# State space mixer: step sizes in the exponents, rows and their exponentials fetched on GpSimd's queue, all groups in one strand

## The chip, the cores and the metric

One core of one Trainium2 chip runs the whole kernel in one launch. The metric is the device time of one execution in microseconds (us); lower is better. Time of before: 1747.45 us, the median of 3 runs (1746.28 to 1748.42). The engines are PE (TensorE, matmuls), DVE (VectorE), ACT (ScalarE), POOL (GpSimd) and SP (SyncE, which here only issues transfers). PEld is PE's loading of weights. Each engine carries out its own instructions in the order in which they stand in its program; an instruction that must wait holds up those behind it.

## The reference

Two layers of a hybrid block over 256 latent and 256 context tokens (D_MODEL 1024): a shared input projection, a bidirectional state space mixer and an attention mixer beside each other, gates, an output projection, and a feed-forward part. The change touches only the state space mixer, in chunks of 128 tokens, with 16 heads in 4 groups. Per direction it computes:

```python
xd = (xs * dt[..., None]).reshape(bsz, nc, SSD_CHUNK, g, r, p)
a = (dt * a_head).reshape(bsz, nc, SSD_CHUNK, g, r).transpose(0, 3, 4, 1, 2)
a_cs = jnp.cumsum(a, axis=-1)
cb = jnp.einsum('bclgn,bcsgn->bgcls', cc, bc)
decay_in = jnp.exp(segsum(a))
y_diag = jnp.einsum('bgcls,bgrcls,bcsgrp->bclgrp', cb, decay_in, xd)
...
y_off = jnp.einsum('bclgn,bcgrpn,bgrcl->bclgrp', cc, h_in, jnp.exp(a_cs))
y = (y_diag + y_off).reshape(bsz, n, n_heads, p)
```

Here a is the step size times a negative number, and segsum gives a_cs[l] - a_cs[s] where s <= l and minus infinity elsewhere. So the output of a chunk is a part inside the chunk (the matrix cb * decay * dt, applied to xs) and a part from the state h_in that enters it. The second direction does the same on the reversed tokens; both are summed.

## The kernel before, in words

**Matrix products.** Every large product is done with both operands split into a high and a low part (three matmuls for one). Weight blocks of 128x1024 come by SP's queue (load_w, L304), ACT casts the high part whi (L313), DVE subtracts for the low part wlo (L314). `gemm_f` (L393 to L410) runs the matmuls of a block and calls `pump()` after every 6 of them. `pump()` moves two lists of generators, `lanes[0]` and `lanes[1]`, on by one step each. Whatever such a step issues to PE is kept at that place of PE's program (`pmm`, `ptr`, L84 to L88). The instructions of the other engines are put in order by a scheduler, ahead of time; they need not follow the order of the code.

**The state space stage.** In each layer it runs beside 10 blocks of GEMM columns: four blocks XS (the input xs, evacuated with a 3-tap convolution, L568 to L572, and a gate by tanh, L665 and L666), two blocks GS, four blocks Z. Layer 0 has 4 chunks of 128 (N = 512), layer 1 has 2 (N = 256); with 4 groups that is 16 and 8 items (group g, chunk t).

**States** (`states`, in lane 0, one generator per group): transposes xs and B to xT (psssT, L910) and bT, then six times: xd = xT * ddt on POOL (L925), a matmul psstate, and the new state h = h * etot + psstate on DVE (L935, L938) or a copy on ACT (L933).

**Outputs** (`outputs`, in lane 1, one generator per group, started when its states have xT). An item's cumulative sums a_cs stand as rows in DRAM (csd, written on POOL's queue at L861). `fetch` brings eight rows, broadcast to all 128 partitions: 512 KB by SP's queue (L952, two buffers). `head` then does: the product pscb on PE; its copy under the two triangular masks, cbm (DVE L961); cc = exp(cs) (ACT L966); cs minus the column's own sums csc (POOL L969, once for each direction); their minimum (DVE L972) and its exponential E (ACT L974); cc * CF (DVE L975). The item's own step then makes X: per head, cbm times the step size of the one direction (ACT L991) plus cbm times that of the other (DVE L992), and then X * E (DVE L993). The 12 (or 8, where a direction has no state coming in) matmuls pyyd take xT with X and h_in with cc.

Of the 2 buffers for cs, one is free again when E has been used in X * E.

**Around it.** Before the stage, a small part computes the step sizes dt, ddt, csc, csd and etot for all heads of a layer (L822 to L864); the attention, gates and the attention's output projection lie between it and the stage.

## Time and profile before

| | |
|---|---|
| median of 3 runs | 1747.45 us (1746.28 to 1748.42) |
| the profiled execution, its own time | 1740.01 us |
| its span (first to last instruction) | 1738.2 us |
| mean granted clock of PE | 0.993 |
| PE / DVE / ACT / POOL busy | 96% / 66% / 49% / 10% |
| state space stage of layer 0 | 406.8 to 577 us of the span |
| state space stage of layer 1 | 1346.4 to 1477 us |
| 512 KB fetches cs<-csd | 24, on SP's queue, median 5.8 us from issue to landing |

How the rows of the profile are read. A row of a group: line, engine, operation, output<-inputs, shapes, count | busy us, mean ns of one | idle time of the engine just before them, and who ended it. A row of a tile: ns min/median/max, first and last start. A row of the waits: who waited for whom, us in total, times, longest. A row of the windows: the stretch, its length, busy us of PE, PEld, DVE, ACT, POOL (with counts), the granted clock, the share of the DMA engines, GB/s. A row of the timeline: start, duration, engine, line, and in brackets the idle time before it and who ended it. A row of the transfers: issuing queue, count, KB each, median us to landing. A few per cent of the matmul records are missing.

### The profile page before, as it was taken

How to read it: one execution, taken by the hardware profiler on the slowest of the kernel's cores; microseconds unless marked ns; L12 is line 12 of the kernel's file. 1: busy time of each engine (PE TensorE's matmuls, PEld its weight loads, DVE VectorE, ACT ScalarE, POOL GpSimd, SP SyncE). 2: the span in 40 equal slices, each digit the busy share in tenths (PEclk: the TensorE clock that was granted, in tenths of full speed). 3: DMA queues.
4: the chain of work that ended last, by engine and by line, in shares of the span. 5: the costliest groups of instructions: out<-in, count | busy, mean ns of one | idle time of the engine just before them, and what ended most of it. 6: DMA issues, size and time to landing. Idle time of an engine off the chain costs nothing. (4 is left out here: it accounts for less than half of the span.)

```text
span 1738.2 us, 27022 instructions
## 1 busy us (share of the span) xinstructions
PE 1667.1 (96%) x10547; PEld 1406.2 (81%) x10547; DVE 1148.0 (66%) x2008; ACT 848.2 (49%) x1567; POOL 181.3 (10%) x212
## 2 busy tenths in 40 slices
PE   7999999999988999999999999999999898989997
PEld 4788878777766788888888888788879788989997
DVE  4776667325988855766666326666675789779964
ACT  3565665413545423644444225555655455466653
POOL 3000010001433000300000002100000252010000
PEclk9999999999999999999999999999999999989999
DMA  9644333555443234233323335844535445646653
GB/s 317 215 127 126 115 119 108 166 173 146 121 107 100 74 109 146 74 97 97 97 87 95 92 108 161 255 146 146 152 93 171 121 110 144 199 154 185 193 176 117
DMA packets 233199, 240.71 MB, mean 138 GB/s; under 512 B 10908, under 2 KB 223551, under 8 KB 233071
## 3 DMA queue, kind: packets, MB, share of 16 engines
q1 hardware_dynamic: 230720, 237.14, 45.4%
q8 instruction: 83, 1.36, 0.3%
q0 software_dynamic: 1312, 1.03, 0.2%
q10 hardware_dynamic: 1039, 0.81, 0.1%
q14 instruction: 45, 0.37, 0.1%
HBM read 234.62 MB, written 4.33 MB: 137 GB/s over the span
## 5 line engine op out<-in xcount | busy, mean ns | idle before, releaser
L314 DVE TENSOR_TENSOR wlo<-raw,whi 128x1024 fp32r<-128x1024 f32 (+1 forms) x318 | 388.3, 1221 | 255.7 <-ACT whi L313 254.8
L313 ACT CAST whi<-raw 128x1024 fp32r<-128x1024 f32 (+1 forms) x318 | 329.2, 1036 | 378.4 <-PE pmmmm L408 146.6
L407 PE MATMUL pmmmm<-th,whi 128*128 128x512 f32 x744 | 306.3, 412 | 1.6 <-DVE chv L572 1.6
L408 PE MATMUL pmmmm<-tl,whi 128*128 128x512 f32 x744 | 296.5, 399 | 0.0
L409 PE MATMUL pmmmm<-th,wlo 128*128 128x512 f32 x744 | 295.6, 397 | 0.0
L407 PEld LDWEIGHTS pmmmm<-th,whi 128*128 128x128 f32 x744 | 140.5, 189 | 42.2 <-issue 7.9
L409 PEld LDWEIGHTS pmmmm<-th,wlo 128*128 128x128 f32 x744 | 140.4, 189 | 34.5 <-issue 1.0
L408 PEld LDWEIGHTS pmmmm<-tl,whi 128*128 128x128 f32 x744 | 140.5, 189 | 31.0 <-issue 2.2
L393 PE MATMUL pmmmm<-th,whi 128*128 128x256 f32 x480 | 138.5, 289 | 1.5 <-ACT whi L313 1.3
L395 PE MATMUL pmmmm<-th,wlo 128*128 128x256 f32 x480 | 134.7, 281 | 0.6 <-DVE wlo L314 0.6
L394 PE MATMUL pmmmm<-tl,whi 128*128 128x256 f32 x480 | 134.8, 281 | 0.0
L969 POOL TENSOR_TENSOR cs<-cs,csc 128x512 f32<-128x512 f32 x48 | 69.1, 1454 | 264.0 <-DMA cs<-csd 141.5
L393 PEld LDWEIGHTS pmmmm<-th,whi 128*128 128x128 f32 x480 | 90.7, 189 | 6.2 <-issue 3.8
L394 PEld LDWEIGHTS pmmmm<-tl,whi 128*128 128x128 f32 x480 | 90.8, 189 | 0.7 <-issue 0.4
L395 PEld LDWEIGHTS pmmmm<-th,wlo 128*128 128x128 f32 x480 | 90.6, 189 | 0.8 <-DVE wlo L314 0.8
L409 PE MATMUL psmm<-th,wlo 128*128 128x512 f32 x200 | 79.3, 397 | 0.0
L725 ACT ACTIVATE e<-psscore,nmx 128x512 f32<-128x512 f32 (+1 forms) x96 | 58.1, 610 | 43.5 <-DVE nmx L722 40.5
L408 PE MATMUL psmm<-tl,whi 128*128 128x512 f32 x200 | 79.2, 396 | 0.0
L521 POOL TENSOR_TENSOR rs<-ms,mhalf 128x2 f32<-128x2 f32 x9 | 6.3, 699 | 698.5 <-DVE ms L518 698.5
L407 PE MATMUL psmm<-th,whi 128*128 128x512 f32 x200 | 79.0, 395 | 0.0
L722 DVE TENSOR_REDUCE nmx<-psscore 128x1 f32<-128x512 f32 (+1 forms) x80 | 51.8, 684 | 34.3 <-PE psscore L85 34.2
L441 PE MATMUL pmmmm<-whi,th 128*128 128x256 f32 x256 | 74.3, 290 | 0.0
(346 smaller groups left out, 3899.0 us busy)
## 6 DMA issues: line engine op xcount, KB each, us to landing
raw<-in_w_in_dram SPq DMA_DIRECT2D x124, 512.0 KB, 4.0
raw<-in_w_up_dram SPq DMA_DIRECT2D x88, 512.0 KB, 3.6
mraw<-in_w_mod_dram SPq DMA_DIRECT2D x80, 512.0 KB, 4.7
raw<-in_w_down_dram SPq DMA_DIRECT2D x45, 512.0 KB, 3.6
cs<-csd SPq DMA_DIRECT2D x24, 512.0 KB, 5.8
boot<-in_w_mod_dram SPq DMA_DIRECT2D x16, 512.0 KB, 9.3
raw<-in_w_br_att_dram SPq DMA_DIRECT2D x16, 512.0 KB, 3.6
raw<-in_w_br_ssd_dram SPq DMA_DIRECT2D x16, 512.0 KB, 3.5
```

The costliest lines, as they stand in the source:

```text
L313: pin(A.copy(hi[:, 0:n, :], raw[:, 0:n, :]))
L314: pin(V.tensor_tensor(lo[:, 0:n, :], raw[:, 0:n, :], hi[:, 0:n, :].bitcast(F32), op=ALU.subtract))
L393: T.matmul(o[f], whi[:, kk, cs], xh, start=first, stop=False)
L394: T.matmul(o[f], whi[:, kk, cs], xl, start=False, stop=False)
L395: T.matmul(o[f], wlo[:, kk, cs], xh, start=False, stop=last)
L407: T.matmul(o, whi[:, k % 4, cs], hi[k][:, 0:n], start=k == 0, stop=False)
L408: T.matmul(o, whi[:, k % 4, cs], lo[k][:, 0:n], start=False, stop=False)
L409: T.matmul(o, wlo[:, k % 4, cs], hi[k][:, 0:n], start=False, stop=k == k_tiles - 1)
L441: T.matmul(b[:, n, :], hi[k][:, ts], whi[:, k % 4, :], start=k == 0 and n == 0, stop=False)
L722: V.tensor_reduce(nmx[:, cc, 0:ng], sc[cc].rearrange("p (g k) -> p g k", g=ng), axis=AX.X, op=ALU.max, negate=True)
L725: A.activation(e[cc][:, g * w:(g + 1) * w], sc[cc][:, g * w:(g + 1) * w], AF.Exp, bias=nmx[:, cc, g:g + 1], accum_out=sm[:, cc, g:g + 1])
L969: G.tensor_tensor(cs[:, dr], cs[:, dr], csc[:, t, 16 * dr + 4 * g:16 * dr + 4 * g + 4].unsqueeze(2).to_broadcast([P, 4, P]), op=ALU.subtract)
```

## The change

1. **Step sizes in the exponents.** csc becomes ln(max(dt, 1e-37)) minus the column's cumulative sum. Per direction, exp(row + csc) is then dt times the decay. The triangular masks become `far`, a tile with 0 inside and -1e30 outside, made once, which POOL adds to the fetched rows (new L979, once for each direction). ACT takes the exponentials head by head with csc as bias, 8 of 128x128 (new L985), and copies pscb to cb (new L981). DVE adds the two directions (new L998) and makes X by one product with cb (new L999).
2. **Two tables in DRAM.** Beside csd's rows their exponentials (ecr) are written; cc is fetched ready-made and only multiplied by CF (DVE, new L1001). A layer's writes on POOL's queue go from 8 to 16 in layer 0 and stay 8 in layer 1.
3. **GpSimd's queue.** Both fetches, 512 KB each, are issued from POOL (new L970): the rows with three buffers and three items ahead, the exponentials with two buffers and two items ahead.
4. **One strand.** One `outputs` generator goes through all items of the layer and is started before the XS blocks; it waits before an item's output matmuls until that group's states are done.
5. **States in pairs.** Both directions' xd are issued in one step, 11 steps rather than 14 for a group.

```diff
-        csd = dp.tile([4, 2, 16, P], F32, name=f"csd{i}")
+        csd = [dp.tile([4, 2, 16, P], F32, name=f"csd{i}_{n}") for n in range(2)]
...
+            V.tensor_scalar(u, dtT[:, :, 0:32], 1e-37, None, op0=ALU.max)
+            A.activation(u, u, AF.Ln)
...
-                V.tensor_copy(csc[:, :, cs], p1v[:, dr, :, cs])
+                V.tensor_tensor(csc[:, :, cs], u[:, :, cs], p1v[:, dr, :, cs], op=ALU.subtract)
...
+            A.activation(ecr, p3[:, 0:256], AF.Exp)
-            for t in range(4):
+            for t in range(NT):
...
-                    G.dma_start(csd[t, dr], csr[r:r + 16, dr * P:(dr + 1) * P])
+                    for n, src in enumerate((csr, ecr)):
+                        G.dma_start(csd[n][t, dr], src[r:r + 16, dr * P:(dr + 1) * P])
...
-                cs = up.tile([P, 2, 4, P], F32, tag="cs", name=nm("cs"), bufs=2)
-                nc.sync.dma_start(cs.rearrange("p d h l -> p d (h l)"),
+                d = up.tile([P, 2, 4, P], F32, tag=("cs", "cc")[n], name=nm("rows"), bufs=(3, 2)[n])
+                G.dma_start(d.rearrange("p d h l -> p d (h l)"),
...
-                V.tensor_tensor(cbm, cb[:, 0:P].unsqueeze(1).to_broadcast([P, 2, P]), tri2, op=ALU.mult)
-                A.activation(cc[:, d0:d1], cs[:, d0:d1], AF.Exp)
                 for dr in range(2):
-                    G.tensor_tensor(cs[:, dr], cs[:, dr],
-                                    csc[:, t, 16 * dr + 4 * g:16 * dr + 4 * g + 4].unsqueeze(2).to_broadcast([P, 4, P]),
-                                    op=ALU.subtract)
-                V.tensor_tensor(cs[:, 0], cs[:, 0], cs[:, 1], op=ALU.min)
-                A.activation(E, cs[:, 0], AF.Exp)
+                    G.tensor_tensor(cs[:, dr], cs[:, dr], far[:, dr, :].unsqueeze(1).to_broadcast([P, 4, P]), op=ALU.add)
+                A.copy(cb, pc[:, 0:P])
+                for dr in range(2):
+                    for h in range(4):
+                        c = 16 * dr + 4 * g + h
+                        A.activation(cs[:, dr, h, :], cs[:, dr, h, :], AF.Exp, bias=csc[:, t, c:c + 1])
...
-                for h in range(4):
-                    A.activation(X[:, h, :], cbm[:, 0, :], AF.Copy, scale=dcol[0])
-                    V.scalar_tensor_tensor(X[:, h, :], cbm[:, 1, :], dcol[1], X[:, h, :], op0=ALU.mult, op1=ALU.add)
-                V.tensor_tensor(X, X, E, op=ALU.mult)
+                V.tensor_tensor(cs[:, 0], cs[:, 0], cs[:, 1], op=ALU.add)
+                V.tensor_tensor(X, cs[:, 0], cb.unsqueeze(1).to_broadcast([P, 4, P]), op=ALU.mult)
+                V.tensor_tensor(ccv, ccv, CF[g][:, tsl].unsqueeze(1).to_broadcast([P, 4 * len(dirs), P]), op=ALU.mult)
+                if n + 3 < len(items):
+                    sums.append(fetch(*items[n + 3], 0))
...
+                if n + 2 < len(items):
+                    grown.append(fetch(*items[n + 2], 1))
...
+        lanes[1].append(outputs())
         for g in range(4):
...
-            lanes[1].append(outputs(g, sh))
```

**How the instructions move.** Three places. First, GpSimd at the start of layer 0's stage. Before: the subtractions of items 0 and 1 (cs_4044, cs_4067), then xd of group 0.

```order
L969 TENSOR_TENSOR cs_4044<-cs_4044,csc_622 128x512 [waits DMAHW2_49,DMAHW3_49,DMAHW1_49,DMAHW4_49,DMAHW0_49,DMAHW5_49,DVE_49,DMAHW6_49,PE_49,DMAHW7_49,Activation_49,Pool_49]
L969 TENSOR_TENSOR cs_4044<-cs_4044,csc_622 128x512
L969 TENSOR_TENSOR cs_4067<-cs_4067,csc_622 128x512 [waits DMAHW4_49,Activation_49]
L969 TENSOR_TENSOR cs_4067<-cs_4067,csc_622 128x512
L925 TENSOR_TENSOR xd_4040<-xT_4008,ddt_624 128x256 [waits DVE_49]
L925 TENSOR_TENSOR xd_4083<-xT_4008,ddt_624 128x256
L925 TENSOR_TENSOR xd_4122<-xT_4008,ddt_624 128x256 [waits PE_49]
```
After, from the mask additions of item 2 on (rows_3939): rows_3975 and rows_4295 are the rows of items 3 and 4, of which the first waits for X of item 0 and the second for X of item 1 (DVE); xd_4099 is the first xd of group 0.

```order
L979 TENSOR_TENSOR rows_3939<-rows_3939,far 128x512 [waits DMASW6_49]
L979 TENSOR_TENSOR rows_3939<-rows_3939,far 128x512
L970 DMA rows_3975<-csd_0_625 128x2x512 [waits DMASW1_49,DVE_49,DMASW2_49,Activation_49,Pool_49]
L970 DMA rows_4295<-csd_0_625 128x2x512 [waits DVE_49,Activation_49,Pool_49]
L979 TENSOR_TENSOR rows_3975<-rows_3975,far 128x512 [waits DMASW1_49]
L979 TENSOR_TENSOR rows_3975<-rows_3975,far 128x512
L979 TENSOR_TENSOR rows_4295<-rows_4295,far 128x512 [waits DMASW2_49]
L979 TENSOR_TENSOR rows_4295<-rows_4295,far 128x512
L937 TENSOR_TENSOR xd_4099<-xT_4067,ddt_627 128x256 [waits DMAHW4_49,DMAHW3_49,DMAHW5_49,DMAHW2_49,DMAHW6_49,DMAHW1_49,DMAHW7_49,DMAHW0_49,DVE_49]
L937 TENSOR_TENSOR xd_4101<-xT_4067,ddt_627 128x256
```
The two fetches and four mask additions of items 3 and 4 stand ahead of the first xd, where nothing of a later item than 1 stood.

Second, ScalarE in the running items of layer 0. Before, item 6: cc and E from the fetched cs_4573, and the four scaled copies into X_4681, which wait for DVE's cbm.

```order
L966 ACTIVATE cc_4628<-cs_4573 128x512 [waits DMAHW1_49]
L916 COPY bT_4620<-psssT_4615 128x512 [waits PE_49]
L974 ACTIVATE cs_4573<-cs_4573 128x512 [waits DVE_49]
L991 ACTIVATE X_4681<-cbm_4626,dtT_621 128x128 [waits DVE_49]
L313 CAST whi_4668<-raw_4660 128x1024 [waits DMAHW7_49,PE_49]
L933 COPY h_4643<-psstate_4641 128x256 [waits PE_49]
L1028 ACTIVATE gs_1_3883<-pmmmm_4559 128x512
L991 ACTIVATE X_4681<-cbm_4626,dtT_621 128x128 x3
```
After: rows_4471 are the rows of item 6; cb_4407 and cb_4483 are the copies for the X of items 3 and 4.

```order
L981 COPY cb_4407<-pscb_4403 128x128 [waits PE_49]
L569 ACTIVATE chv_4438<-pmmmm_4364,cols_158 128x512 [waits PE_49]
L668 ACTIVATE cth_4437<-chv_4438 128x512 [waits DVE_49,Activation_49]
L314 CAST whi_4520<-raw_4358 128x1024 [waits DMAHW6_49,PE_49]
L985 ACTIVATE rows_4471<-rows_4471,csc_624 128x128 [waits DMASW6_49,Pool_49]
L985 ACTIVATE rows_4471<-rows_4471,csc_624 128x128 x3
L985 ACTIVATE rows_4471<-rows_4471,csc_624 128x128 [waits Pool_49]
L981 COPY cb_4483<-pscb_4479 128x128 [waits PE_49]
L985 ACTIVATE rows_4471<-rows_4471,csc_624 128x128 x3
```
The copy of cb for item 4 stands behind five exponentials of item 6. In the same way cb_4407 (item 3) comes just behind all eight of item 5.

Third, VectorE at the start of layer 0's stage, up to xs_1. Before:

```order
L571 SCALAR_TENSOR_TENSOR chv_3939<-pmmmm_3913,cols_157,chv_3939 128x2x255 [waits Activation_49]
L572 SCALAR_TENSOR_TENSOR chv_3939<-pmmmm_3913,cols_157,chv_3939 128x2x255 [waits DVE_49]
L666 SCALAR_TENSOR_TENSOR xs_0_3874<-cth_3938,chv_3939 128x512 [waits Activation_49]
L314 TENSOR_TENSOR wlo_3980<-raw_3895,whi_3979 128x1024 [waits DMAHW5_49,PE_49,Activation_49]
L975 TENSOR_TENSOR cc_4060<-cc_4060,CF_0_617 128x1024 [waits Activation_49]
L972 TENSOR_TENSOR cs_4044<-cs_4044 128x512 [waits DMAHW3_49,Pool_49]
L571 SCALAR_TENSOR_TENSOR chv_3971<-pmmmm_3945,cols_157,chv_3971 128x2x255 [waits Activation_49]
L314 TENSOR_TENSOR wlo_3998<-raw_3977,whi_3997 128x1024 [waits DMAHW7_49,PE_49,Activation_49]
L572 SCALAR_TENSOR_TENSOR chv_3971<-pmmmm_3945,cols_157,chv_3971 128x2x255 [waits DVE_49]
L910 COPY xT_4008<-psssT_4009 128x4x128 [waits PE_49]
L972 TENSOR_TENSOR cs_4067<-cs_4067 128x512 [waits DMAHW4_49,Pool_49]
L666 SCALAR_TENSOR_TENSOR xs_1_3875<-cth_3970,chv_3971 128x512 [waits Activation_49]
```
After: rows_3941 and rows_3943 are the fetched exponentials of items 0 and 1, rows_3935 and rows_3937 their rows; X_3971 and X_4291 are the X of items 0 and 1.

```order
L1001 TENSOR_TENSOR rows_3941<-rows_3941,CF_0_619 128x1024 [waits DMASW7_49]
L573 SCALAR_TENSOR_TENSOR chv_3998<-pmmmm_3928,cols_158,chv_3998 128x2x255 [waits DVE_49]
L1001 TENSOR_TENSOR rows_3943<-rows_3943,CF_0_619 128x1024 [waits DMASW0_49]
L998 TENSOR_TENSOR rows_3935<-rows_3935 128x512 [waits DMASW4_49,Activation_49,Pool_49]
L999 TENSOR_TENSOR X_3971<-rows_3935,cb_3955 128x512 [waits DVE_49]
L998 TENSOR_TENSOR rows_3937<-rows_3937 128x512 [waits DMASW5_49,Activation_49,Pool_49]
L669 SCALAR_TENSOR_TENSOR xs_0_3889<-cth_3997,chv_3998 128x512 [waits Activation_49]
L572 SCALAR_TENSOR_TENSOR chv_4030<-pmmmm_4004,cols_158,chv_4030 128x2x255 [waits Activation_49]
L999 TENSOR_TENSOR X_4291<-rows_3937,cb_3987 128x512 [waits DVE_49]
L573 SCALAR_TENSOR_TENSOR chv_4030<-pmmmm_4004,cols_158,chv_4030 128x2x255 [waits DVE_49]
L315 TENSOR_TENSOR wlo_4039<-raw_3910,whi_4038 128x1024 [waits DMAHW5_49,PE_49,Activation_49]
L669 SCALAR_TENSOR_TENSOR xs_1_3890<-cth_4029,chv_4030 128x512 [waits Activation_49]
```
The products with both fetched exponentials, two sums and an X come ahead of xs_0; the evacuation of xs_1 follows the second X.

More of the change, by code (lines that the diff above doesn't have):

```diff
@@ L644, in hybrid_backbone_kernel @@
                         row = boot_mod(raws)
+            V.tensor_scalar(far, kt[:, C_LE:C_LE + 2 * P].rearrange("p (d l) -> p d l", d=2), -1.0, 1e30,
+                            op0=ALU.add, op1=ALU.mult)
             load_rest(0, nc.scalar)
@@ new lines, in states @@
+            for n in range(3):
+                pair_ = [q for q in todo if q[0] == n]
+                xds = []
+                for _, dr, t, nxt in pair_:
+                    xd = up.tile([P, 4, 64], F32, tag="xd", name=nm("xd"), bufs=2)
+                    G.tensor_tensor(xd, xT[:, t, :].rearrange("p (h q) -> p h q", h=4),
+                                    ddt[:, t, 16 * dr + 4 * g:16 * dr + 4 * g + 4].unsqueeze(2).to_broadcast([P, 4, 64]),
+                                    op=ALU.mult)
+                    xds.append(xd)
+                yield 1
+                for (_, dr, t, nxt), xd in zip(pair_, xds):
+                    s = bank("s", "state")[:, 0:256]
+                    pmm(s, bT[:, t * P:(t + 1) * P], xd.rearrange("p h q -> p (h q)"), start=True, stop=True)
+                    new = up.tile([P, 256], F32, tag="h", name=nm("h"), bufs=10)
+                    if n == 0:
+                        A.copy(new, s)
+                    else:
+                        V.tensor_tensor(new.rearrange("p (h q) -> p h q", h=4), cur[dr].rearrange("p (h q) -> p h q", h=4),
+                                        etot[:, t, 16 * dr + 4 * g:16 * dr + 4 * g + 4].unsqueeze(2).to_broadcast([P, 4, 64]),
+                                        op=ALU.mult)
+                        V.tensor_tensor(new, new, s, op=ALU.add)
+                    cur[dr] = new
+                    h_in[dr, nxt] = new
+                    yield 1
@@ L1010, in outputs @@
                                 start=False, stop=dr == dirs[-1])
-                yield 1
-            for f in range(2):
-                j = 2 * g + f
-                V.scalar_tensor_tensor(xs[j][:, 0:N], xs[j][:, 0:N], L["D"][:, j:j + 1], yb[f][:, 0:N],
-                                       op0=ALU.mult, op1=ALU.add)
-            done.append(g)
-            yield 1
+                if n + 2 < len(items):
+                    grown.append(fetch(*items[n + 2], 1))
+                if t == NT - 1:
+                    for f in range(2):
+                        j = 2 * g + f
+                        V.scalar_tensor_tensor(xs[j][:, 0:N], xs[j][:, 0:N], L["D"][:, j:j + 1], yb[f][:, 0:N],
+                                               op0=ALU.mult, op1=ALU.add)
+                    done.append(g)
+                yield 1
+                yield 1
+        lanes[1].append(outputs())
         for g in range(4):
```

94 lines of the change are left out of this document (37 added, 57 removed).

## The prediction

> **What bounds the kernel now.** I read the page of the profile first (busy time by engine), then PE's waits in the two stretches that the change touches, then the busy time in those stretches, and last the stalls one by one.
>
> ```profile
> core 0: 1738.2 us, clock 0.993
> PE 1667.1 (96%) x10547; PEld 1406.2 (81%) x10547; DVE 1148.0 (66%) x2008; ACT 848.2 (49%) x1567; POOL 181.3 (10%) x212
> 406.80:577.00 170.20, 153.12 (x917) 119.68 (x914) 140.51 (x239) 83.31 (x163) 60.31 (x56) 0.98 0.43 112
> 1346.40:1477.00 130.60, 120.56 (x852) 104.67 (x851) 109.28 (x184) 67.60 (x121) 44.36 (x40) 0.99 0.46 124
> ```
>
> PE is the bound: 96% busy. The last two rows are the scan stages of layer 0 and of layer 1 (length, then busy us of PE, PEld, DVE, ACT, POOL, then the clock). In layer 0 PE is idle for 170.20 - 153.12 = 17.1 us, in layer 1 for 10.0 us. Nothing else that the change touches can give time back, so a gain ends near 27 us and what the clock lost after the stalls; a loss has no such end. Who made PE wait (us in total, times, longest), layer 0 and then layer 1:
>
> ```profile
> PE pyyd L85 <- DVE X L993: 8.2, 7, 2.1
> PE psstate L85 <- POOL xd L925: 6.5, 4, 3.4
> PE psssT L88 <- DVE xs L666: 2.1, 1, 2.1
> ...
> PE psssT L88 <- DVE xs L666: 2.9, 1, 2.9
> PE pyyd L85 <- DVE h L938: 1.6, 1, 1.6
> PE pmmmm L407 <- DVE chv L572: 1.6, 1, 1.6
> PE psstate L85 <- DVE h L938: 1.4, 1, 1.4
> PE pmmmm L393 <- ACT whi L313: 1.3, 1, 1.3
> PE psstate L85 <- POOL xd L925: 1.0, 1, 1.0
> ```
>
> Layer 0's start costs 2.1 + 0.2 = 2.3 us (rows below) and the rest, 17.0 - 2.3 = 14.7 us, is X and xd in the running items. Layer 1's start costs 2.9 + 1.6 = 4.5, the rest 5.3.
>
> **What an item costs PE.** The layer has 10 blocks of GEMM columns beside the scan, 480 matmuls.
>
> ```profile
> 344.99 0.39 PE L408 MATMUL pmmmm<-tl,whi 128*128 128x512 f32 x1
> ...
> 346.15 0.40 PE L407 MATMUL pmmmm<-th,whi 128*128 128x512 f32 x1
> ```
>
> Five matmuls in 346.15 - 344.99 = 1.16 us: 0.232 each, 111.4 us for 480. The stage's other 153.12 - 111.4 = 41.7 us are the 16 items' own, 2.6 each. After the change the order gives an item 24 GEMM matmuls (6 ahead of its output matmuls, 18 behind), 5.6 us, so PE comes round to the next item after 5.6 + 2.6 = **8.2 us**. That is what the other engines must keep up with. In layer 1 it is 120.56 / 8 = 15 us.
>
> **The new loop.** Its parts, by the nearest rows of before:
>
> ```profile
> L969 POOL TENSOR_TENSOR cs<-cs,csc x32: 1034/1079/2082, 417.8 to 570.5; 128x512 f32<-128x512 f32 x32
> L972 DVE TENSOR_TENSOR cs<-cs x16: 675/686/1518, 420.9 to 572.0; 128x512 f32<-128x512 f32 x16
> L993 DVE TENSOR_TENSOR X<-X,cs x16: 674/682/1530, 433.6 to 574.8; 128x512 f32<-128x512 f32 x16
> DMA to landing us min/median/max: 4.9/5.7/8.8
> fwb<-in_final_norm_w_dram POOLq DMA_DIRECT2D x1, 512.0 KB, 6.1
> raw<-in_w_up_dram SPq DMA_DIRECT2D x88, 512.0 KB, 3.6
> L969 POOL TENSOR_TENSOR cs<-cs,csc 128x512 f32<-128x512 f32 x32 | 42.6, 1346 | 183.6 <-DMA cs<-csd 141.5 <-ACT cc L966 25.3 <-DVE X L993 7.9
> L991 ACT ACTIVATE X<-cbm,dtT 128x128 f32<-128x128 f32 x64 | 20.8, 391 | 8.4 <-DVE cbm L961 8.3
> ```
>
> By the code the fetch for item n+3 may go as soon as X(n) is made, nearly three items early. By the order it isn't early: ScalarE's copy of cb(n+1), which X(n+1) needs, stands behind the first five or six exponentials of item n+3. These wait for both mask additions on GpSimd, which wait for the fetch, which waits for X(n). So every X waits for a fetch released by the X before: landing + two mask additions + the last one or two exponentials + the copy + the product. The landing is bounded by 4.9 (shortest broadcast of this size on SP's queue) and 8.8; I take 6.1, the one 512 KB broadcast on GpSimd's own queue. The additions (same shape and engine as L969) take 2 x 1.03 to 2 x 2.08; mean 2 x 1.35. Sum: 6.1 + 2.7 + 0.6 + 0.4 + 0.7 = **10.5 us** against 8.2. With the shortest of each, 4.9 + 2.1 + 0.4 + 0.4 + 0.7 = 8.5. There are 11 such links (fetch 5 to X 3, up to fetch 15 to X 13): 11 x (10.5 - 8.2) = **+25.3 us**, in place of the 14.7 of before (the old waits for X and xd lie inside the new ones).
>
> The Trainium skill, DMA: Bandwidth & Descriptors, "Anatomy of one DMA — SWDGE (gpsimd) path", fits a transfer from this queue as 2.0 us plus the bytes at 436 GB/s, an estimate of 3.2 us for 512 KB. The trace has 6.1 for the one such broadcast; by the page's figure the loop would be 7.6 us and cost nothing.
>
> **The start of the stage.** Now five fetches stand ahead of it where two stood, and on VectorE two products of fetched rows (c0, c1), two sums and an X come before xs_0.
>
> ```profile
> 408.00:412.00 4.00, 4.00 (x18) 3.21 (x18) 0.00 (x0) 0.00 (x0) 0.00 (x0) 1.00 1.06 339
> 412.00:416.00 4.00, 4.00 (x19) 3.19 (x18) 1.70 (x3) 1.65 (x3) 0.00 (x0) 1.00 1.02 303
> 415.79 0.69 DVE L666 SCALAR_TENSOR_TENSOR xs<-cth,chv 128x512 f32<-128x512 f32 x1 [0.76 <-ACT cth L665]
> 422.97 1.40 DVE L314 TENSOR_TENSOR wlo<-raw,whi 128x1024 fp32r<-128x1024 f32 x1
> 424.29 0.73 DVE L572 SCALAR_TENSOR_TENSOR chv<-pmmmm,cols,chv 128x510 f32<-128x510 f32 x1
> 426.75 1.21 DVE L975 TENSOR_TENSOR cc<-cc,CF 128x1024 f32<-128x1024 f32 x1
> 426.88 0.66 PE L88 MATMUL psssT<-kt,xs 128*128 128x128 f32 x4 [2.10 <-DVE xs L666]
> 429.31 0.70 PE L85 MATMUL psstate<-xd,bT 128*128 128x256 f32 x2 [0.16 <-POOL xd L925]
> ```
>
> The transfers are already full there (339 and 303 GB/s, the last column): 2.6 MB in these 8 us, 1.05 of it the two old fetches. Five fetches (2.6 MB) and the other 1.5 MB take 4.1 / 0.321 = 13 us, so the last lands between 421 and 425; I take 422.7. Then c1's product 1.2, sum, X and sum 2.1, xs_0 0.7 (ends 426.7), and chv, X, chv, wlo, xs_1 4.1: xs_1 is there at 430.8. Its transposes would run at 424.8 without a stall: 6.0 us late. Next, xd of the first group stands behind the mask of item 4, whose fetch waits for X(1) at 428.1: + 0.5 to issue + 6.1 landing + 2.7 + 0.6 = 438.0, where PE is ready at 429.3 - 2.3 + 6.0 = 433.0: another 5.0. Together 11.0 instead of 2.3: **+8.7 us**. In layer 1 xd stands behind item 3's mask only, about 2.1 us earlier: 6.0 + 2.9 = 8.9 instead of 4.5, +4.4. There PE's 15 us per item hide the loop, and of the other 5.3 us of stalls I count 3 as gone, since the states are now spread evenly: **+1.4** in layer 1.
>
> **What costs nothing.** VectorE loses the masked copy and four multiply-adds per item:
>
> ```profile
> L992 DVE SCALAR_TENSOR_TENSOR X<-cbm,dtT,X 128x128 f32<-128x128 f32 x64 | 23.6, 415 | 1.2 <-ACT X L991 1.2
> L961 DVE TENSOR_TENSOR cbm<-pscb,kt 128x256 f32<-128x256 f32 x16 | 6.7, 416 | 0.1
> L966 ACT ACTIVATE cc<-cs 128x1024 f32<-128x1024 f32 (+1 forms) x16 | 13.5, 841 | 18.0 <-DMA cs<-csd 12.4 <-PE pscb L85 3.1 <-PE pyyd L85 2.5
> L974 ACT ACTIVATE cs<-cs 128x512 f32<-128x512 f32 x16 | 10.1, 630 | 30.9 <-DVE cs L972 30.9
> ```
>
> That is 30 us busy in layer 0, but VectorE was busy for 140.51 of 170.20 and will wait for fetches instead. The minimum becomes an addition of the same shape. ScalarE trades two wide exponentials and four copies (0.84 + 0.63 + 4 x 0.39 = 3.0 us) for nine small operations (9 x 0.39 = 3.5): 0.5 us more an item, with 83 of 170 us in use; should that cover go, 8 us. The states run in pairs: three rounds fewer per group. If PE waited for xd alone, up to 6.5 us would be in it. SP's queue no longer holds fetches in front of weights, worth at most the 1.3 us of whi above. The doubled writes of the rows (16 for 8 in layer 0) fall in an empty stretch of GpSimd:
>
> ```profile
> 248.82 3.91 POOL L861 DMA_DIRECT2D csd<-csr  x8 [3.66 <-ACT csr L857]
> 300.68 1.03 POOL L756 TENSOR_TENSOR rsa<-ss,mhalf 128x4 f32<-128x4 f32 x1 [47.95 <-DVE ss L754]
> ```
>
> They add 4 us in a gap of 48. In the running items the two fetch issues, 0.5 us each at this row's rate, fit between GpSimd's work (60 of 170 us).
>
> After the long stalls of before, PE's clock fell:
>
> ```profile
> 515.00:520.00 5.00, 5.00 (x36) 3.94 (x35) 4.50 (x13) 1.88 (x7) 0.00 (x0) 0.69 0.56 159
> 525.00:530.00 5.00, 2.52 (x22) 2.19 (x24) 3.77 (x7) 3.01 (x9) 3.59 (x5) 0.84 0.02 9
> 530.00:535.00 5.00, 5.00 (x26) 3.93 (x23) 4.02 (x8) 2.38 (x5) 2.19 (x3) 0.82 0.45 67
> ```
>
> 5 x (0.31 + 0.16 + 0.18) = 3.2 us lost. I leave it: stalls of the same length remain.
>
> **Sum**: 25.3 - 14.7 + 8.7 + 1.4 = +20.7. The profiled execution took 1740.0, so 1760.7; the median of the runs is 7.4 us above that execution, so **1768 us**.
>
> **Rivals.**
> 1. *The prefetch closes the loop* (faster). It turns at 8.2 us, that is at a landing of 3.8 or less with the other parts as taken. For it: plain 512 KB loads on SP's queue land in 3.6 (the raw row), which makes 8.0. Against it: every broadcast took at least 4.9. Then the 14.7 and the 3.2 go, the start costs +4.6 (its fetches still share full transfers), layer 1 -1.5: -14.8, **1733**. The Trainium skill's 3.2 us, from the section named above, would make this the likeliest case; no run here shows it for a broadcast.
> 2. *It cancels.* Landing near 4.9 and unhindered additions, 8.5 us: 11 x 0.3 = 3.3, start +6, -14.7, layer 1 +0.5: -5, **1742**; with 0.6 us a link, no change.
> 3. *Two fetches share the transfer engines* (slower still). The row exponentials of item n+2 are issued right behind, and VectorE has their product ahead of X. Halfway from 6.1 to the longest landing, 7.4: 11.8 a link, 39.6 in all, start and layer 1 +12: +37, **1784**.
>
> **Chances.** My forecast 0.46 (1757 to 1778), rival 1 0.24, rival 2 0.12, rival 3 0.18. A run tells about 0.2% (3.5 us) from no change. Rival 2 is split 0.05 faster and 0.07 same; with 0.01 of the forecast the same is 0.08: faster 0.29, same 0.08, slower 0.63. The range, 1731 to 1788, reaches past the centres of both outer cases and leaves out about half of rival 1 and a fifth of rival 3. My forecast's own range is 1757 to 1778.
>
> **What would show it.** Right: in layer 0 PE waits for X some eleven times at about 2 us, the copy of cb ends just behind exponentials that waited for GpSimd, GpSimd is idle before the mask additions for landings of 6 us, and the first psstate comes near 438. The start is wrong if xs_0 (415.79 above) begins before 420, the loop if landings are under 4 us or if the gaps between output matmuls are 8.2. The whole is wrong if PE's idle time in layer 0's stage is under 17 us.

## The result, and the profile after

The changed kernel takes **1789.48 us** (median of 4 runs, 1787.74 to 1794.5) beside 1747.93 for the kernel before in the same session: a ratio of 1.0243, with an interval of 1.0220 to 1.0265. It is slower, as forecast, but by 41.5 us and not by 20.7, and 1.5 us outside the range. The profiled execution took 1789.51, 49.5 more than that of before. Of these 49.5, some 8 are the choice of execution: the profile of after is at the median of its kernel, that of before 7.4 us under its own (1747.45).

The page of after (span and clock, busy time by engine):

```profile
core 0: 1787.7 us, clock 0.980
PE 1677.3 (94%) x10547; PEld 1411.9 (79%) x10547; DVE 1100.6 (62%) x1891; ACT 848.2 (47%) x1643; POOL 219.2 (12%) x268
```

The two state space stages of after in the windows: length, then busy us of PE, PEld, DVE, ACT and POOL, the clock, the share of the transfer engines, GB/s.

```profile
406.00:625.00 219.00, 177.48 (x998) 136.83 (x996) 119.71 (x179) 89.90 (x222) 83.97 (x89) 0.91 0.54 135
1380.00:1524.50 144.50, 122.87 (x846) 105.28 (x844) 93.39 (x146) 65.94 (x145) 56.26 (x57) 0.96 0.54 142
```

The same two stretches of before, drawn to the same statistics matmul at the end:

```profile
406.80:592.00 185.20, 167.71 (x982) 131.05 (x978) 150.42 (x256) 88.58 (x173) 61.01 (x57) 0.98 0.43 114
1346.40:1478.90 132.50, 121.81 (x861) 105.72 (x859) 110.33 (x186) 68.21 (x122) 45.05 (x41) 0.99 0.46 124
```

VectorE did save its work (150.42 to 119.71 us), and it bought nothing. PE's idle time in layer 0 went from 185.20 - 167.71 = 17.5 us to 41.5, in layer 1 from 10.7 to 21.6. PE is also busy for longer with the same matmuls, since the clock fell: 0.98 to 0.91 in layer 0. Measured between the same two instructions (in layer 0 from a gate's product at 362.97 or 363.95 to a statistics matmul at 592.15 or 625.02), layer 0's part is 31.9 us longer (24.0 of it stalls; the rest is for the most part the clock, which is reckoned in another way further down), that of layer 1 11.8. The other 5.8 lie outside both stages, in code that is the same. The low profile of before could account for them, which is not shown, since it is the only profile of that kernel.

Who made PE wait after (us in total, times, longest), the longest waits of layer 0:

```profile
PE pscb L85 <- DVE xT L919: 12.8, 2, 6.7
PE pmmod L466 <- DMA mraw<-in_w_mod_dram: 10.4, 2, 9.2
PE pyyd L85 <- DVE X L999: 4.5, 3, 2.2
```

and of layer 1 (xT is the transposed xs, bT the transposed B, mraw a weight block for the modulation, chv the convolved xs ahead of its gate):

```profile
PE psstate L85 <- POOL xd L937: 8.0, 4, 3.8
PE psssT L88 <- DVE xs L669: 6.6, 1, 6.6
```

In layer 0 X itself is named only three times. PE runs ahead on GEMM matmuls while X is late, until something that stands behind X in VectorE's program (the copy xT of a group's transposes, L919) is due: the lateness of several items comes out as one stall, of 6.1 us at 499 and of 6.7 us at 548. Before, no stall in this stage was longer than 3.4.

**The loop, one turn.** The timeline of after, GpSimd's part, then ScalarE's, then VectorE's, from X of one item to X of the next:

```profile
483.72 1.46 POOL L970 DMA_DIRECT2D rows<-csd  x2 [2.45 <-DVE X L999]
489.42 2.52 POOL L979 TENSOR_TENSOR rows<-rows,far 128x512 f32<-128x512 f32 x2 [4.23 <-DMA rows<-csd]
...
490.72 1.65 ACT L985 ACTIVATE rows<-rows,csc 128x128 f32<-128x128 f32 x5 [4.19 <-POOL rows L979]
492.28 0.24 ACT L981 COPY cb<-pscb 128x128 f32<-128x128 f32 x1
...
482.75 0.68 DVE L999 TENSOR_TENSOR X<-rows,cb 128x512 f32<-128x512 f32 x1
492.49 1.23 DVE L1001 TENSOR_TENSOR rows<-rows,CF 128x1024 f32<-128x1024 f32 x1 [4.70 <-DMA rows<-csd]
493.64 0.68 DVE L999 TENSOR_TENSOR X<-rows,cb 128x512 f32<-128x512 f32 x1
```

X at 482.75 releases the fetch at 483.72, which lands by 489.42; the masks follow, five exponentials, the copy of cb right behind them (492.28), and X at 493.64. It is the forecast's loop, called a ring below: a closed chain in which each X waits for a fetch that the X before released. One link was left out of its sum: VectorE's product of the *second* fetched table stands ahead of X (1.15 us from its start to X). That product waited for its own landing until 492.49, and the copy of cb ended at 492.52, so in this turn the two came at the same time.

**The start of layer 0**, in the windows of after:

```profile
412.00:416.00 4.00, 4.00 (x19) 3.25 (x19) 0.75 (x1) 0.93 (x2) 0.58 (x1) 1.00 0.88 191
416.00:420.00 4.00, 3.68 (x16) 2.62 (x14) 0.00 (x0) 2.53 (x8) 2.18 (x3) 1.00 0.92 182
420.00:424.00 4.00, 0.64 (x8) 0.16 (x8) 0.00 (x0) 2.50 (x8) 2.73 (x3) 1.00 0.92 188
424.00:428.00 4.00, 0.00 (x0) 0.00 (x0) 1.72 (x2) 0.00 (x0) 2.00 (x2) 0.68 0.80 209
```

Two of the stalls there, in the timeline of PE, and the first product with fetched exponentials and xs_0 in that of VectorE:

```profile
430.68 1.08 PE L466 MATMUL pmmod<-mraw,s 128*32 128x256 f32 x8 [9.16 <-DMA mraw<-in_w_mod_dram]
...
444.62 0.70 PE L85 MATMUL psstate<-xd,bT 128*128 128x256 f32 x2 [2.75 <-POOL xd L937]
...
426.28 1.23 DVE L1001 TENSOR_TENSOR rows<-rows,CF 128x1024 f32<-128x1024 f32 x1 [10.82 <-DMA rows<-csd]
...
432.01 0.68 DVE L669 SCALAR_TENSOR_TENSOR xs<-cth,chv 128x512 f32<-128x512 f32 x1
```

The transfer engines are 0.9 busy while they move only 182 to 191 GB/s, where the forecast counted on 321. A weight load of SP's queue (mraw), issued at 409.44, then comes 9.2 us late, and VectorE waits 10.82 us for the exponentials of item 0, with xs_0 behind them. In these rows PE idles through the whole of 424 to 428.

### The profile page after: what moved, and what is told of

Same layout as the page of the kernel before. It is cut to its first block, busy times and chain, and to the rows that moved or that the text cites. A ratio compares the mean times of both kernels' runs of the same rounds, so it can differ in the third digit from the quotient of the medians.

```text
span 1787.7 us, 27019 instructions
## 1 busy us (share of the span) xinstructions
PE 1677.3 (94%) x10547; PEld 1411.9 (79%) x10547; DVE 1100.6 (62%) x1891; ACT 848.2 (47%) x1643; POOL 219.2 (12%) x268
## 5 line engine op out<-in xcount | busy, mean ns | idle before, releaser
L408 PE MATMUL pmmmm<-th,whi 128*128 128x512 f32 x744 | 311.0, 418 | 0.0
L985 ACT ACTIVATE rows<-rows,csc 128x128 f32<-128x128 f32 x192 | 62.1, 391 | 91.4 <-POOL rows L979 91.1
```

The source lines that it names most:

```text
L408: T.matmul(o, whi[:, k % 4, cs], hi[k][:, 0:n], start=k == 0, stop=False)
L985: A.activation(cs[:, dr, h, :], cs[:, dr, h, :], AF.Exp, bias=csc[:, t, c:c + 1])
```

## The experiments

Seven edits were put on the changed kernel, alone and together. One table first; "X to X" is the mean time from X of item 3 to X of item 13 in layer 0, a tenth of the difference of two rows of the timeline. It tells how fast X is made and not whether PE waits for it: before itself has 9.7 (465.98 to 563.36), and e10 with 9.5 is faster than e12 with 9.2. So it is read beside PE's idle time. Gains in us below are differences of these medians; the ratios, taken against runs of before on the same chip, put them up to some 3 us apart from that.

| kernel | what is edited in after | median us | ratio to before (interval) | X to X |
|---|---|---|---|---|
| after | - | 1789.48 | 1.0243 (1.0220, 1.0265) | 11.75 |
| e1 | ScalarE's copy pinned ahead of its exponentials | 1786.04 | 1.0238 (1.0209, 1.0266) | 10.85 |
| e2 | fetches issued by SP | 1779.88 | 1.0199 (1.0172, 1.0226) | 11.0 |
| e5 | e1 + e2 | 1750.28 | 1.0018 (1.0001, 1.0035) | 8.45 |
| e12 | VectorE's three operations pinned | 1763.48 | 1.0112 (1.0084, 1.0141) | 9.2 |
| e8 | e1 + e12 | 1757.10 | 1.0063 (1.0041, 1.0084) | 9.4 |
| e6 | e1 + masks on VectorE | 1761.09 | 1.0082 (1.0058, 1.0106) | 9.8 |
| e4 | one fetch | 1755.69 | 1.0053 (1.0035, 1.0071) | 9.9 |
| e3 | strand started later | 1791.69 | 1.0262 (1.0230, 1.0294) | 11.7 |
| e7 | first fetches wait for xs_0 | 1785.28 | 1.0217 (1.0195, 1.0239) | 11.6 |
| e11 | e5 + e7 | 1743.09 | 0.9989 (0.9973, 1.0004) | 8.7 |
| e9 | e11, first five fetches on GpSimd | 1748.28 | 1.0017 (1.0002, 1.0031) | 8.5 |
| e10 | e9 + e12 | 1743.80 | 0.9987 (0.9972, 1.0001) | 9.5 |
| e14 | e5 + one fetch | 1736.53 | 0.9951 (0.9933, 0.9968) | 8.8 |
| e13 | e11 + one fetch | 1735.70 | 0.9942 (0.9925, 0.9959) | 8.6 |

### e1: the copy ahead of the exponentials

The pinned instructions of an engine keep the order of the code, so that ScalarE copies cb of an item before that item's eight exponentials. This is meant to cut the forecast's ring at ScalarE and nothing else.

```diff
-                A.copy(cb, pc[:, 0:P])
+                tc.keep_in_program_order(A.copy(cb, pc[:, 0:P]))
...
-                        A.activation(cs[:, dr, h, :], cs[:, dr, h, :], AF.Exp, bias=csc[:, t, c:c + 1])
+                        tc.keep_in_program_order(A.activation(cs[:, dr, h, :], cs[:, dr, h, :], AF.Exp, bias=csc[:, t, c:c + 1]))
```

> ScalarE's copies of cb and its head-by-head exponentials keep the order of the code, so the copy for item n+1 no longer stands behind exponentials of item n+3; all else as in the changed kernel. Loop theory (every X waits for the fetch that the X before released, about 11.6 us an item): the 27.7 us of PE stalls that fall in the running items of layer 0 go for the most part, and half of the clock lost there, about -30 us: near 1760. Queue theory (GpSimd's queue itself is slow) and start theory (the five fetches at the start of a stage): no change, 1785 to 1793.

Measured: 1786.04, 3 us less than after (0.05% by the ratios, inside their intervals). The ring of the forecast cannot be the whole cause. The result is where the expectation had put the queue and the start; e2 and e7 below speak against these. The timeline of e1, GpSimd and then VectorE, shows another ring:

```profile
521.85 2.53 POOL L979 TENSOR_TENSOR rows<-rows,far 128x512 f32<-128x512 f32 x2 [5.60 <-DMA rows<-csd]
524.31 1.45 POOL L970 DMA_DIRECT2D rows<-csd  x2
...
536.83 0.72 POOL L970 DMA_DIRECT2D rows<-csd  x1 [1.18 <-DVE X L999]
...
530.17 1.23 DVE L1001 TENSOR_TENSOR rows<-rows,CF 128x1024 f32<-128x1024 f32 x1 [8.93 <-DMA rows<-csd]
535.57 0.69 DVE L999 TENSOR_TENSOR X<-rows,cb 128x512 f32<-128x512 f32 x1
```

GpSimd waits 5.60 us for a landing to add the masks, and only behind them does it issue the next two fetches (524.31). VectorE waits 8.93 us for the landing of an exponentials' table, with the next X queued behind the product; and that X (535.57) releases GpSimd's next fetch (536.83). GpSimd issues late because it computes in between, VectorE makes X late because the product stands ahead of it. The forecast's third rival named half of this ("VectorE has their product ahead of X").

### e2: the fetches issued by SP

This takes GpSimd out of the second ring and leaves the first as it is.

```diff
-                G.dma_start(d.rearrange("p d h l -> p d (h l)"),
+                nc.sync.dma_start(d.rearrange("p d h l -> p d (h l)"),
```

> Both fetches are issued on SP's queue, as before the change; nothing else is edited. Queue theory: broadcasts land in under 5 us, the mod weights no longer come 9 us late at the start of layer 0, -20 us or more: below 1770. Loop theory: the loop stays (by the order the copy of cb(n+1) still stands behind exponentials of item n+3), landings stay at 5 to 6 us, and weights now wait on SP behind fetches: 1780 to 1800.

Measured: 1779.88, 10 us less than after; X to X 11.0. In ScalarE's program the copy of item 3 still stands behind the exponentials of item 5, as in after, so the first ring is closed still. The queue itself did not make the fetches slow: with SP they took 7.9 us in the median, with GpSimd 7.0. The 48 fetches of e2:

```profile
DMA to landing us min/median/max: 5.2/7.9/16.0
```

### e5: both

> The edits of the pinned copy and of SP's queue together. Queue-order theory (in GpSimd's program a mask addition that waits for a landing stands ahead of the next fetch's issue, so that two landings follow each other in every item; it took over when the copy was pinned, and the copy's loop remained when only the queue was changed): with both gone the stalls of the running items in layer 0 fall from 27.7 us to under 12, 1750 to 1765. Product theory (VectorE's product with a fetched table waits for its landing, with X, the low weight parts and the transposed xs queued behind it): that order is untouched, 1772 to 1785.

The edit is that of e1 and that of e2, no more:

```diff
+                nc.sync.dma_start(d.rearrange("p d h l -> p d (h l)"),
...
+                tc.keep_in_program_order(A.copy(cb, pc[:, 0:P]))
```

Measured: 1750.28, 39 us less than after. Alone the edits gave 3 and 10. X of item 3 is the one at 482.75 in the turn of after that is shown above; X of item 13, in the same timeline:

```profile
600.20 0.68 DVE L999 TENSOR_TENSOR X<-rows,cb 128x512 f32<-128x512 f32 x1
```

Both in e1:

```profile
481.13 1.12 DVE L999 TENSOR_TENSOR X<-rows,cb 128x512 f32<-128x512 f32 x1
589.65 0.69 DVE L999 TENSOR_TENSOR X<-rows,cb 128x512 f32<-128x512 f32 x1
```

In e2:

```profile
479.40 0.68 DVE L999 TENSOR_TENSOR X<-rows,cb 128x512 f32<-128x512 f32 x1
589.48 0.68 DVE L999 TENSOR_TENSOR X<-rows,cb 128x512 f32<-128x512 f32 x1
```

In e5:

```profile
476.66 1.12 DVE L999 TENSOR_TENSOR X<-rows,cb 128x512 f32<-128x512 f32 x1
561.12 0.68 DVE L999 TENSOR_TENSOR X<-rows,cb 128x512 f32<-128x512 f32 x1
```

That is 117.5, 108.5, 110.1 and 84.5 us for ten items. Two rings of nearly the same length lie beside each other; with one of them open the other sets the pace, and only with both open does an item take 8.45 us, close to the 8.2 that the forecast gave to PE alone. PE's idle time in layer 0's stage says the same: 41.5 us in after, 32.9 in e1, 35.2 in e2, 14.2 in e5. Layer 0 of e5 in the windows:

```profile
406.00:589.00 183.00, 168.79 (x997) 131.23 (x996) 131.40 (x178) 89.93 (x222) 69.21 (x58) 0.96 0.63 161
```

And what is left of PE's waits there:

```profile
PE pmmmm L408 <- DVE chv L573: 7.1, 1, 7.1
PE pmmod L466 <- DMA mraw<-in_w_mod_dram: 2.5, 1, 2.5
PE pscb L85 <- DVE xT L919: 2.2, 2, 1.2
PE pyyd L85 <- DVE X L999: 1.5, 2, 0.9
```

The running items wait for 3.7 us (14.7 before the change); 9.6 are the start (2.3 before), and layer 1's start has another 8.2 and 2.5. So the change as meant does save the old waits, and loses them again at the starts of the stages: the ratio of e5 is 1.0018 (1.0001 to 1.0035).

### e12, e8, e6: the second ring opened at other places

e12 keeps VectorE's sum, X and product in the order of the code, X ahead of the product (VectorE's three operations of the table):

```diff
-                V.tensor_tensor(cs[:, 0], cs[:, 0], cs[:, 1], op=ALU.add)
-                V.tensor_tensor(X, cs[:, 0], cb.unsqueeze(1).to_broadcast([P, 4, P]), op=ALU.mult)
+                tc.keep_in_program_order(V.tensor_tensor(cs[:, 0], cs[:, 0], cs[:, 1], op=ALU.add))
+                tc.keep_in_program_order(V.tensor_tensor(X, cs[:, 0], cb.unsqueeze(1).to_broadcast([P, 4, P]), op=ALU.mult))
...
-                V.tensor_tensor(ccv, ccv, CF[g][:, tsl].unsqueeze(1).to_broadcast([P, 4 * len(dirs), P]), op=ALU.mult)
+                tc.keep_in_program_order(V.tensor_tensor(ccv, ccv, CF[g][:, tsl].unsqueeze(1).to_broadcast([P, 4 * len(dirs), P]), op=ALU.mult))
```

> Only VectorE's sum, X and product keep the order of the code; ScalarE is not pinned, both fetches and the masks stay on GpSimd. By the order the scheduler now also puts the copy for item n ahead of all but the exponentials of item n+1 in most items, so both rings open with one edit. Ring theory: 1753 to 1762, as with both pinned. If the copy has to be pinned as well: 1775 or more.

Measured: 1763.48, 26 us less than after by one edit on VectorE. This is not a clean cut of one ring: the scheduler answered it by moving ScalarE's copies too. The copy of item 3 now stands behind the exponentials of item 4 and no longer of item 5, and that of item 4 behind those of item 5, whose fetch X of item 2 releases, so the first ring gives two items per turn. Its 26 us are both rings eased, and the run does not tell them apart.

e8 is e12 with the pin of e1:

```diff
+                tc.keep_in_program_order(A.copy(cb, pc[:, 0:P]))
...
+                tc.keep_in_program_order(V.tensor_tensor(X, cs[:, 0], cb.unsqueeze(1).to_broadcast([P, 4, P]), op=ALU.mult))
```

> The pinned copy, and on VectorE the sum, X and the product with the fetched exponentials keep the order of the code, so X of an item comes ahead of that item's product; both fetches and the mask additions stay on GpSimd. Product theory: X no longer waits for the second landing, -15 to -25 against the pinned copy alone: 1762 to 1772. Queue-order theory: GpSimd's program is as before, 1780 to 1790.

Measured: 1757.10, 29 less than e1. The second ring is thus opened on VectorE nearly as well as by the queue; e8 stays 7 us above e5. PE's largest wait there beside mraw is for xd, 7.5 us in three times; xd stays in GpSimd's program among masks that await landings.

e6 has the pin of e1, and moves the masks to VectorE, so that GpSimd computes nothing between its fetches but xd:

```diff
-                    G.tensor_tensor(cs[:, dr], cs[:, dr], far[:, dr, :].unsqueeze(1).to_broadcast([P, 4, P]), op=ALU.add)
+                    V.tensor_tensor(cs[:, dr], cs[:, dr], far[:, dr, :].unsqueeze(1).to_broadcast([P, 4, P]), op=ALU.add)
```

> The pinned copy, and the mask additions on VectorE rather than GpSimd; both fetches stay on GpSimd's queue, where now nothing waits for a landing. Queue-order theory: as with SP's queue, 1755 to 1770 (the start of the stage stays). Product theory: VectorE now waits for both landings with everything behind it, 1785 to 1800. If slowness lay in GpSimd's transfers as such: 1780 or more, with landings over 6 us.

Measured: 1761.09, 25 less than e1. This speaks for the mask additions in GpSimd's program as what holds the next fetch; the landings of the rows are now waited for on VectorE too, and an item takes 9.8 us, not 8.45.

### e4: one fetch

ScalarE makes the exponentials from the fetched rows, as before the change; the second table is never fetched.

```diff
+                cc = up.tile([P, 2, 4, P], F32, tag="cc", name=nm("cc"), bufs=2)
+                dd = reach(t)[1]
+                A.activation(cc[:, dd], cs[:, dd], AF.Exp)
+                grown.append(cc)
...
-            grown = [fetch(*items[n], 1) for n in range(2)]
+            grown = []
...
-                if n + 2 < len(items):
-                    grown.append(fetch(*items[n + 2], 1))
```

> No second fetch: cc is made by ScalarE from the fetched rows, as before the change; the second table is still written but not read. Bytes theory (two broadcasts per item fill the transfer engines and VectorE's product with the fetched one delays X): landings at the start fall from 11.5 us to under 8, the mod weights come in time, loop shorter by the 1.2 us product: -20 us or more. Loop theory: the order of the copies loosens only in part (the copies of items 4 is ahead of item 6's exponentials, that of item 5 is behind item 7's), so -5 to -15.

Measured: 1755.69, 34 us less than after, with GpSimd's queue, the masks and ScalarE's order left free. There is no second ring without a second table, the median landing falls from 7.0 to 6.4 us, and the start of layer 0 takes 6.0 us of stalls where after has 13.1. Of all single edits this one gives back the most. It is no clean cut either: the scheduler moved ScalarE's copies here too. That of item 4 stands ahead of the exponentials of item 6 (in after it is behind five of them), while that of item 5 still stands behind two of item 7, so the first ring is eased in part as well.

### e3 and e7: the start

e3 starts the strand behind the first XS blocks in the code:

```diff
-        lanes[1].append(outputs())
         for g in range(4):
...
             lanes[0].append(states(g, sh))
+            if g == 0:
+                lanes[1].append(outputs())
```

> The strand of outputs is started after the first XS blocks (with the states of group 0) and not ahead of them; nothing else is edited. Start theory: the first 13.1 us of stalls in layer 0 and the 8 to 10 in layer 1 go, with the 4 and 2 us of clock behind them, less some 5 us for a first item that comes later: -15 to -22, 1768 to 1774. Loop theory alone: the loop runs as before, no more than -5.

Measured: 1791.69, no gain. It did not test what it was made for: the fetches depend on nothing in those blocks, kept their place in GpSimd's program and went out as early; PE waited for mraw for 10 us again. e7 adds a true dependence: the first five buffers are touched by a copy of a column of xs_0 before the fetch.

```diff
+            born = []
+
             def fetch(g, t, n):
...
+                if len(born) < 5:
+                    V.tensor_copy(d[:, 0, 0, 0:1], xs[0][:, 0:1])
+                    born.append(1)
```

> The strand starts after the first XS blocks, and each of the first five fetches is made to wait for xs_0 by a one-column copy of xs_0 into its buffer (overwritten by the fetch); nothing else is edited. Start theory: the waits for the mod weights (10.3 us in layer 0) and for xs in layer 1 (6.6 us) go, with 4 us of clock: -12 to -20, 1770 to 1778. If the first item's lateness costs as much as that: 1784 to 1792.

Measured: 1785.28. The wait for mraw is gone, chv waits 6.2 us instead, and the running items turn as slowly as before (11.6): a better start is worth 4 us here, where 12 to 20 were expected of it.

### e11, e9, e10: start and rings together

e11 is e5 with e7. In e9 only the five first fetches are on GpSimd's queue; e10 is e9 with the pins of e12.

```diff
+                first = len(born) < 5
+                if first:
+                    V.tensor_copy(d[:, 0, 0, 0:1], xs[0][:, 0:1])
+                    born.append(1)
+                (G if first else nc.sync).dma_start(d.rearrange("p d h l -> p d (h l)"),
```

> As the kernel with the first five fetches by GpSimd after xs_0, but these five are issued by SP too. In SP's program the next weights stand behind the fetches that wait for xs_0. If that holds the weights up: 4 to 10 us slower than with GpSimd. If the weights are early enough: the same within 3 us.

> Pinned copy; the strand starts after the first XS blocks; the first five fetches are issued by GpSimd and wait for xs_0 (by a one-column copy), all later ones by SP. Ring theory (two rings through ScalarE, GpSimd and VectorE, each closed by the order of one engine; the start is a third, separate cost that shows fully only when the rings are open): against the pinned copy with SP's queue (1750) the 9.6 and 10.6 us of waits at the two starts fall to under 4 each, -8 to -16: 1734 to 1743, faster than the kernel before. If moving the start only moves the waits to the first items: 1746 to 1754.

> As the kernel with the first five fetches by GpSimd after xs_0, with VectorE's sum, X and product kept in the order of the code as well. Ring theory: both rings were open already, so the second cut adds nothing: within 4 us of that kernel. If VectorE's product still held X there: -4 to -10 against it.

Measured: 1743.09, 1748.28 and 1743.80: ratios of 0.9989, 1.0017 and 0.9987, whose intervals reach to 1 or within 0.0002 of it. None can be told from before, by the 0.2% that the forecast took as what a run tells. Three expectations missed: e9, which was to be faster than before, still has a wait of 7.2 us for chv at the start of layer 0; e11 is 5 us faster than e9, where it was to be slower or the same within 3; and e10 is 4.5 us under e9, just past the 4 that were allowed if the second cut added nothing. e11 is 7 us under e5 by the medians, with its first fetches later (0.29% by the ratios, whose intervals touch).

### e14 and e13: one fetch with the rings open

e14 is e5 with e4's edit, e13 is e14 with e7's.

```diff
+                nc.sync.dma_start(d.rearrange("p d h l -> p d (h l)"),
...
+                A.activation(cc[:, dd], cs[:, dd], AF.Exp)
+                grown.append(cc)
...
+                tc.keep_in_program_order(A.copy(cb, pc[:, 0:P]))
```

> As the pinned copy with SP's queue (1750), but with one fetch per item (cc made by ScalarE), strand started ahead of the XS blocks as in the changed kernel. Bytes at the start: three fetches land by 417 and not by 425, so xs_0 comes in time and the 9.6 and 10.6 us of starts fall by half: 1738 to 1744. Order at the start (VectorE's products, sums and X ahead of xs_0): 1746 to 1752.

> As the kernel with the first fetches on SP after xs_0 and the pinned copy (1743), but with one fetch per item: cc is made by ScalarE from the rows, three fetches at the start instead of five. If the bytes of the five fetches hold the start of the stages: the 8.1 us of stalls left at layer 0's start and the 6.6 at layer 1's fall to under 4 each, -5 to -10: 1733 to 1738, faster than the kernel before. If the start is held by the order of the engines alone: 1740 to 1746.

Measured: 1736.53 (0.9951, 0.9933 to 0.9968) and 1735.70 (0.9942, 0.9925 to 0.9959): both beat the kernel before and the changed one. The span of e14 is 1734.7 us at a clock of 0.990. Its window of layer 0:

```profile
406.00:590.00 184.00, 173.18 (x1021) 135.34 (x1014) 137.82 (x192) 105.52 (x248) 80.52 (x58) 0.98 0.44 115
```

The row goes on for 6 us behind the statistics matmul at which the one of e5 ends (588.75 there, 583.77 here); PE does not idle in them. PE's waits in it:

```profile
PE pmmod L466 <- DMA mraw<-in_w_mod_dram: 4.3, 2, 3.9
PE pyyd L85 <- DVE X L1003: 3.2, 3, 2.4
PE psstate L85 <- POOL xd L937: 2.6, 3, 2.1
```

Beside e5's window the transfer engines are in use for 0.44 of the stage and not 0.63, and PE idles for 10.8 us and not 14.2. The gain lies at the two starts, whose stalls fall from 9.6 to 4.5 us in layer 0 and from 10.6 to 5.0 in layer 1. One fetch per item (e5 to e14: -13.7 us, 0.67% by the ratios) is worth about twice as much as the same bytes later (e5 to e11: -7.2, 0.29%), and with one fetch the later time adds nothing that can be told (e14 to e13: -0.8, intervals overlap). Whether it is the fewer bytes, or that VectorE no longer waits for a second landing ahead of xs_0, these runs do not tell apart.

## Why the prediction was right and wrong

**The sum by its terms.** In us, forecast and then what the two profiles have: running items of layer 0 +10.6 (25.3 - 14.7) and +13.0 (27.7 - 14.7); start of layer 0 +8.7 and +10.8 (13.1 - 2.3); clock in layer 0 0 and +9.0; layer 1 +1.4 and +11.8; outside the stages 0 and +5.8. The two terms that failed are the clock, which was put at nothing, and layer 1; the first two were a little small. (The clock is an estimate, explained below; the five make 50.4 and not 49.5.)

**Direction, bound and ring: right.** PE stayed the bound, the loss came as PE's idle time in these two stages, and the copy of cb stood behind exponentials that waited for a fetch released by the X before. xs_0 began at 432.01, past the 420 that would have refuted the start, and layer 0's idle time was past 17 us. Of its signs one failed: PE waited for X three times, 4.5 us in all, and not some eleven times at about 2 us; it waited longer for what stands behind X (xT, 12.8 us).

**The loop, 10.5 us a link against 8.2 - mis-sized.** Measured 11.75 against 8.45 (after and e5). PE's pace was right to 3%, if e5 turns at it. The link lacked 1.15 us of VectorE's product, which the forecast kept for a rival, and landings had a median of 7.0 us, where one transfer of before stood for 6.1:

```profile
L970 POOL DMA_DIRECT2D rows<-csd x48: 722/724/787, 407.4 to 1495.8; - x48
...
DMA to landing us min/median/max: 5.0/7.0/18.5
```

Eleven links by 11.75 - 8.45 = 3.3 make 36 us, not 25.3. In the trace they appear as 27.7 us of stalls in the running items; that the rest is PE's slower clock is argued and not shown. An issue on GpSimd also takes 0.72 us, not the 0.5 a piece that the forecast read from small writes.

**One ring - failed as a cause.** The forecast named a single ring through ScalarE; its cure should have given nearly everything back, and gave 3 us (e1). There were two, and a chain of links through three in-order engines stayed closed until both were cut. That 25.3 comes near the 27.7 us of stalls is luck: the second ring, of which the forecast did not know, is of nearly the same length as the first.

**The start, +8.7: near in size, with part of the path missing.** Measured 13.1 us of stalls where 11.0 were forecast. The step "4.1 / 0.321 = 13 us" took the rate of a stretch of before in which two fetches stood among weight loads; with five, the engines were 0.9 full at under 200 GB/s. The forecast's chain through VectorE was there and 6 us later than forecast (xs_0 at 432.01 and not 426.0, the first psstate at 444.62 and not 438). But what PE met first was a weight load on SP's queue, which the forecast did not have. e7, in which that wait is gone and chv waits 6.2 us instead, shows that the two lie beside each other.

**"I leave it: stalls of the same length remain" - failed.** They kept neither their length nor their number: lateness of several items gathers into stalls of 6.1 and 6.7 us, and the start has one of 9.2. Layer 0 lost 11.9 us to the clock by PE's busy time times the missing share of the clock in windows of 5 us, 2.9 before: +9.0 where the forecast had nothing. Four windows of after, and two matmuls behind the stall of 2.75 us that ended at 444.62:

```profile
430.00:435.00 5.00, 4.33 (x16) 2.73 (x17) 4.96 (x9) 2.33 (x5) 1.21 (x2) 0.50 0.22 56
435.00:440.00 5.00, 5.00 (x29) 4.24 (x27) 3.47 (x5) 2.79 (x9) 2.56 (x3) 0.93 0.93 173
...
500.00:505.00 5.00, 2.70 (x7) 1.59 (x7) 1.27 (x2) 2.97 (x10) 4.09 (x4) 0.50 0.83 181
505.00:510.00 5.00, 4.97 (x29) 3.83 (x30) 2.86 (x4) 1.49 (x5) 2.08 (x3) 0.50 0.30 63
...
446.12 0.63 PE L409 MATMUL pmmmm<-tl,whi 128*128 128x512 f32 x1
449.70 0.40 PE L409 MATMUL pmmmm<-tl,whi 128*128 128x512 f32 x1
```

After the stall of 9.2 us PE works at half its clock for a window of 5 us, and after the one of 6.1 us, which ended at 499.34, for two. After the stall of 2.75 us it is slow for about as long as after that of 9.2: a matmul takes 0.63 us and not 0.40, until 449.5. In layer 0 five stalls of after were followed by such slow matmuls (2.75, 4.05, 6.11, 6.67 and 9.16 us) and two of before (2.63 and 3.41); stalls of 2.10 to 2.18 us that met the full clock were not, in either trace. The forecast should have asked how many such stalls there would be. The Trainium skill, TensorE: Matmul & The Clock Gate, Part 1, states that the clock is halved after an idle window of about 3.4 us and restored after as much busy time. These rows agree that the clock is halved after idle time, but here 2.63 us of it were enough.

**Layer 1, +1.4: failed, +11.8, of which 10.9 are stalls.** Its start came out as said (6.6 + 2.1 = 8.7, forecast 8.9). The running items did not: "PE's 15 us per item hide the loop" holds for X, but not for xd. GpSimd and the wait that follows on PE, in after:

```profile
1445.36 2.48 POOL L979 TENSOR_TENSOR rows<-rows,far 128x512 f32<-128x512 f32 x2 [5.37 <-DMA rows<-csd]
1447.80 2.67 POOL L937 TENSOR_TENSOR xd<-xT,ddt 128x256 f32<-128x256 f32 x2
...
1449.51 0.79 PE L85 MATMUL psstate<-xd,bT 128*128 128x256 f32 x1 [3.79 <-POOL xd L937]
```

xd stands behind masks that await a landing. The forecast saw this at the start of the stage, and did not carry it to every item.

**Rivals.** The first and the second did not come. The third (1784) came nearest: it had 11.8 us a link, and 11.75 were measured. Of its two reasons, the product ahead of X is seen in the trace; how much the sharing of the transfer engines adds to a link is not told apart. **Left open**: the 5.8 us outside the stages; what the states in pairs bring, which was not tried alone; and whether the second table's bytes or its ring costs more, since no kernel fetched it without using it.

## What to carry to other kernels

When a change lets an engine both compute on fetched data and issue the next fetch, write down every in-order program on the way from a result to the fetch that it releases and back, and count *all* closed chains: with two of nearly one length, curing one shows almost nothing. A prefetch distance in the code says nothing of this; the place of each instruction in its engine's program does. Price stalls by their number too, and not only by what they add up to: here each of 2.6 us or more was followed by some microseconds at half of PE's clock, and those of 2.2 us or less that met the full clock were not.
